# Holding back half of a back projection and placing it between the steps of the next memory attention

## The chip, the cores and the metric

One core of a Trainium2 chip runs the whole kernel. The metric is the device time in microseconds of one execution, and the lower is the better. The engines are PE (matmuls), PEld (its weight loads, which overlap), DVE (VectorE), ACT (ScalarE), POOL (GpSimd) and SP (it issues most DMAs).

## The reference

One block over 1024 tokens of width 1024, in fp32. Three residual stages follow one another:

```
x = x + mixer(norm(x)) @ w_out         8 heads with a top-256 index mask (DSA),
                                       8 heads with compressed, selected, window branches (NSA)
x = x + memory(norm(x), mem)           4 heads of 128 over 256 memory rows:
        q = rms(h @ w_xq); p = softmax(q k^T); o = p v; return o @ w_xo
x = x + square(relu(norm(x) @ w_ff_in)) @ w_ff_out      4096 features
```

The change lies in the second line: `o @ w_xo` is what the kernel calls the back projection, 512 columns in and 1024 out.

## The kernel before, in words

The tokens are eight tiles of 128 rows. After a head that projects the inputs, two streams of work are written out one between the other. `attend` is the mixer's attention, tile after tile. `fill` is everything else that can already be done: later projections, then `four_tiles` (L1207) for tiles 0 to 3, which adds the mixer's output projection (`rows_out`) and the memory attention, then their MLP, then tiles 4 and 5. What remains after the attention is the tail: `between` for tiles 6 and 7 and the MLP of tiles 4 to 7.

Both are Python generators that yield an amount of work after each piece. `together` (L122) takes a piece of `fill` as long as its sum is no more than the attention's sum times a pace, and else a piece of attention. A yielded pair such as `3, PACES[2]` is a gate: no more of `fill` is taken until the attention has begun the tile after that one, and the count starts again there. Gate 3 stands before `rows_out(3)`, since tile 3's attention output must be there. `alternate` (L156) takes from two streams in turn and `take` (L169) takes pieces of a stream until their sum reaches an amount. The result is only the order of the program: the tile scheduler (L81) moves each engine's instructions once more by a timeline of its own, so that the order on an engine is not the program's.

The memory attention of a pair of tiles is in `heads` (L1048). `w_xq` is multiplied first and leaves four items (two chunks of two heads for two tiles). `steps` then yields five times: after the transposes of all four, after the scores of chunk 0 (L1105 takes their maximum on DVE, L1109 the exponents on ACT), after those of chunk 1, and after the values of each chunk (L1126 transposes, L1141 copies). Score tiles and back projections both take the PSUM tag `D`, which has two banks.

The back projection is `made["xo", t0]`, a `gemm` (L385) with four chunks of 256 columns for two tiles, so eight items. Each is eight matmul records of whole fp32 on PE, 128x256, two groups of four (`psD<-wlo,xl`, `psD<-whi,xl`; the halves of a chunk's weights come raw into two rings, L314, 256 KB each), and one add into the residual rows on DVE (L1041). Each yields 4 x 4 x 256 / 2400 = 1.707.

The mixer's attention works at the same time. The top-k of its index (L770 to L772) is a chain on ACT: 32 bits per tile, each a pass over the scores (L770) and two one-column steps (L771, L772). L777 to L786 end it on DVE. In the stretches spoken of here it is tile 4's chain of 32, and its mask is needed only for tile 4's own DSA scores.

Of the kernel before, what the change touches and what calls it, by code (L numbers as in the profile page):

```python
# [155 lines left out]
def alternate(*streams):  # L156
    streams = list(streams)
    i = 0
    while streams:
        i %= len(streams)  # L160
        w = next(streams[i], None)
        if w is None:
            streams.pop(i)
        else:
            i += 1
            yield w


def take(gen, amount):  # L169
    done = 0.0  # L170
    while done < amount:
        w = next(gen, None)
        if w is None:
            return
        done += w
        yield w


def build(nc, tc, I, C, out):
# [21 lines left out]
    def ring(pool, tag, shape, dt=F32):  # L201
        n = RINGS[pool.name if isinstance(pool.name, str) else "dn"][tag]
        return pool.tile(shape, dt, tag=tag, name=tag, bufs=n)

    def row(ap):
        return ap[None, :]
# [71 lines left out]
    made, behind = {}, []  # L278
# [106 lines left out]
    def gemm(pool, xs, nk, nt, wsrc, chunks, consume, begun=None, keep=None, ks=None):  # L385

        for ci, parts in enumerate(chunks):
            w = sum(n for _, n in parts)
            gr = begun[ci] if begun and ci < len(begun) else list(
                weights(pool, xs, nk, wsrc, parts, None if keep is None else keep + ci, ks))  # L390
            for t in range(nt):
                pt = pst(TAGS[pool.name][0], [P, w])
                for i, k in enumerate(ks or range(nk)):
                    if len(xs) == 1:
                        mm(pt, xs[0](t, k), gr[i][0], i == 0, i == nk - 1)
                        continue
                    wh, wl = gr[i]
                    xh, xl = xs[0](t, k), xs[1](t, k)
                    mm(pt, xh, wh, i == 0, False)
                    mm(pt, xh, wl, False, False)  # L400
                    mm(pt, xl, wh, False, i == nk - 1)
                consume(ci, t, pt)
                yield nk * (5 - len(xs)) * w / 2400.0
# [9 lines left out]
    def xT(pool, nt, whole=False):  # L413

        parts = [pool.tile([P, DM // P, nt * P], F32 if whole else F32R, tag="x" + n, name="x" + n)
                 for n in ("h" if whole else "hl")]
        return (parts, [lambda t, k, x=x: x[:, k, t * P:(t + 1) * P] for x in parts],
                lambda t: [x[:, :, t * P:(t + 1) * P] for x in parts])
# [618 lines left out]
    def residual_add(x2):  # L1037
        def add_to(ci, t, pt):
            w = pt.shape[-1]
            dst = x2[t][:, ci * w:(ci + 1) * w]  # L1040
            v.tensor_tensor(dst, pt, dst, op=ALU.add)  # L1041
        return add_to

    def norm_of(*a):
        norm_T2(*a)
        yield 1.0
# [160 lines left out]
    def four_tiles(pool, x2, made):  # L1207

        four = [[(c * 256, 256)] for c in range(4)]
        room = pool.tile([P, 4, DM], F32, tag="xl", name="xl")  # L1210
        gb2 = [room[:, 3, c * 512:(c + 1) * 512] for c in range(2)]
        begun = {}

        def begin(t):
            o = room[:, t % 2].rearrange("p (k n) -> p k n", n=P)
            for c in (1, 0):
                nc.sync.dma_start(o[:, c * 4:c * 4 + 4, :], oT_dr[t][c])
            if t == 0:
                for u in range(2):
                    x2[u] = ring(pool, "b4", [P, DM])  # L1220
                    nc.sync.dma_start(x2[u], I["x"][0, u * P:(u + 1) * P, :])
                nc.sync.dma_start(room[:, 3], row(W["norm2_g"]).to_broadcast([P, DM]))
            elif t > 1:
                x2[t] = ring(pool, "b4", [P, DM])
                nc.sync.dma_start(x2[t], I["x"][0, t * P:(t + 1) * P, :])
            return [lambda _, k: o[:, k, :]]

        def add(t):
            return lambda ci, _, pt: residual_add(x2)(ci, t, pt)

        def rows_out(t, first=None):
            yield from gemm(pool, begin(t), 8, 1, W["w_out"], four, add(t), first, None, LAST_FIRST)

        def normed(t):
            return norm_of(pool, x2[t], gb2, xt_of(t))

        def memory_heads(t0):
            if t0 == 0:
                xo = room[:, 2].rearrange("p (k n) -> p k n", k=4)
                xo_of = lambda ci: xo[:, ci * 2:ci * 2 + 2, :]  # L1240
            else:
                xs = [ring(pool, "h", [P, 2, 2 * P]) for _ in range(2)]
                xo_of = lambda ci: xs[ci]
            consume_q, made["steps", t0] = heads(pool, 2, lambda ci: [xo_of(ci)], True)
            yield from gemm(pool, [lambda t, k: xf[0](t0 + t, k)], 8, 2, W["w_xq"], [[(0, 256)], [(256, 256)]], consume_q)
            rows = [lambda t, k: xo_of(k // 2)[:, k % 2, t * P:(t + 1) * P]]
            made["xo", t0] = gemm(pool, rows, 4, 2, W["w_xo"], four, lambda ci, t, pt: residual_add(x2)(ci, t0 + t, pt))

        mem_norms, keys, values = memory(pool)
        out0 = rows_out(0)  # L1250
        yield next(out0)
        yield from alternate(mem_norms, out0)
        _, xf, xt_of = xT(pool, 4, True)
        yield from keys
        yield from values
        yield 1, PACES[1]
        yield from alternate(rows_out(1), normed(0))
        yield from normed(1)
        yield from memory_heads(0)
        yield 2, PACES[2]  # L1260
        yield from alternate(made.pop(("steps", 0)), rows_out(2))
        yield from made.pop(("xo", 0))
        yield 3, PACES[2]
        yield from alternate(rows_out(3), normed(2))
        yield from normed(3)
        yield from memory_heads(2)
        yield from made.pop(("steps", 2))
        yield from alternate(made.pop(("xo", 2)), pre_norms(pool, made, x2))

    def pre_norms(pool, made, x2s):  # L1270

        made["x"] = xT(pool, 4)
        made["g"] = gain2(pool, W["norm3_g"])
        for t in range(2):
            yield from norm_of(pool, x2s[t], made["g"], made["x"][2](t))
# [302 lines left out]
    def fill():  # L1578
        for part in range(1, len(PARTS)):
            with tc.tile_pool(name="p2", bufs=1, reuse_waits="tile") as p2:  # L1580
                yield from project(p2, part, late, st)
            projected.append(part)
        pre_pool.__exit__(None, None, None)
        dn = dn_pool.__enter__()
        yield 0, PACES[0]
        x2s, made = {}, {}
        yield from four_tiles(dn, x2s, made)
        yield 3, PACES[3]
        yield from mlp(dn, 0, 4, x2s, made)
        yield 5, PACES[4]  # L1590
        rows = dn.tile([P, 2, 8 * 256], F32, tag="xh", name="xh")
        room = [rows[:, 0, :].rearrange("p (t k n) -> p t k n", t=2, k=8),
                dn.tile([P, 2, 8, 256], F32, tag="xl", name="xl"), rows[:, 1, :].rearrange("p (k n) -> p k n", k=8)]
        yield from between(dn, 4, 2, late["x2s"], False, None, room)
# [53 lines left out]
```

## Time and profile before

| | |
|---|---|
| median of 3 runs | 1666.52 us (1666.29 to 1670.05) |
| the profiled execution | 1667.92 us, span 1666.1 us |
| granted TensorE clock, mean | 0.992 |
| busy share of the span | PE 96%, PEld 85%, DVE 68%, ACT 67%, POOL 57% |
| DMA | 220.73 MB, 132 GB/s on average |

The share of PE says that almost any time won must come from one of the few stretches in which PE is not full. The windows of the trace show where these are; the waits and the timelines say what they wait for.

### The profile page before, as it was taken

Reading aid. Unit: us, or ns where it says so; the run is one execution under the profiler, and the core shown is the slowest. Engines: PE = TensorE matmul, PEld = TensorE weight load, DVE = VectorE, ACT = ScalarE, POOL = GpSimd, SP = SyncE. Lnnn points to the kernel's source line nnn. Section 1 sums busy time; section 2 is a strip of 40 time slices with the busy share of each in tenths; the row PEclk is TensorE's granted clock in tenths of the full one; section 3 lists DMA queues with packets and bytes.
Section 4 is the critical chain, followed back from the end, with each engine's and each line's share of the span. In section 5 each row is a group of like instructions: output and inputs, shape, how many; then the busy total and the mean of one; then the engine's idle time right before and its main releaser. Section 6 shows DMA issues by size and latency. Waiting matters only on the chain.

```text
span 1666.1 us, 29041 instructions
## 1 busy us (share of the span) xinstructions
PE 1604.1 (96%) x9602; PEld 1415.6 (85%) x9602; DVE 1127.0 (68%) x2590; ACT 1109.1 (67%) x2785; POOL 955.5 (57%) x1110
## 2 busy tenths in 40 slices
PE   6998998999999899999999999999998999999999
PEld 6998998788988798888888888888888997887887
DVE  5476779767776984475566665466668657888885
ACT  5455898896599769955998549883555554444443
POOL 2365568545543647777657867571245854554566
PEclk9999999999999999999999999999999999999999
DMA  7975423668444212222222222254268442332354
GB/s 257 307 264 161 149 83 110 227 180 251 135 137 148 78 45 75 78 70 75 70 79 64 69 69 72 71 175 136 86 223 253 150 147 89 103 101 93 100 168 149
DMA packets 184438, 220.73 MB, mean 132 GB/s; under 512 B 24672, under 2 KB 138208, under 8 KB 184288
## 3 DMA queue, kind: packets, MB, share of 16 engines
q1 hardware_dynamic: 176352, 208.39, 39.1%
q0 software_dynamic: 7936, 10.49, 2.4%
q8 instruction: 76, 1.25, 0.3%
q14 instruction: 74, 0.61, 0.1%
HBM read 186.58 MB, written 32.24 MB: 131 GB/s over the span
## 4 chain that ended last, share of the span: by engine, by line
PE 46%; DVE 6%; ACT 4%; POOL 3%; DMA 2%; issue 2%; SPq 0%; ACTq 0%; DVEq 0%; POOLq 0%
PE psD L234 22%; PE psS L234 9%; PE psM L234 5%; PE psPT L234 3%; PE psPV L234 3%; PE psPT L826 3%; POOL wlo L268 2%; DVE wlo L268 2%; DMA wraw<-in_w_ff_out_dram 1%; ACT dmask L770 1%; ACT whi L263 1%; DMA w<-in_w_ff_out_dram 1%; POOL S L816 0%; ACT S L811 0%; DVE P L1481 0%
## 5 line engine op out<-in xcount | busy, mean ns | idle before, releaser
L268 POOL TENSOR_TENSOR wlo<-wraw,whi 128x512 fp32r<-128x512 f32 (+1 forms) x228 | 316.7, 1395 | 198.3 <-ACT whi L263 192.1
L263 ACT ACTIVATE whi<-wraw 128x512 fp32r<-128x512 f32 x329 | 200.3, 626 | 178.0 <-DMA wraw<-in_w_ff_out_dram 37.9
L255 DVE TENSOR_TENSOR pl<-psPT,ph 128x512 fp32r<-128x512 f32 (+1 forms) x232 | 142.4, 620 | 64.8 <-ACT ph L254 63.0
L811 ACT ACTIVATE S<-S,mn 128x128 f32<-128x128 f32 (+7 forms) x192 | 143.1, 746 | 54.8 <-DVE mn L809 53.1
L234 PE MATMUL psD<-whi,h 128*128 128x512 f32 (+1 forms) x480 | 164.1, 397 | 0.5 <-POOL h L1395 0.2
L816 POOL TENSOR_SCALAR S<-S,sums,gi 128x640 f32<-128x640 f32 (+7 forms) x128 | 108.6, 857 | 86.4 <-DVE sums L814 65.8
L254 ACT ACTIVATE ph<-psPT 128x512 fp32r<-128x512 f32 (+1 forms) x232 | 122.9, 539 | 52.1 <-PE psPT L826 45.2
L234 PE MATMUL psD<-xh,wlo 128*128 128x512 f32 (+1 forms) x416 | 145.9, 352 | 0.0
L234 PE MATMUL psD<-xl,whi 128*128 128x512 f32 (+1 forms) x416 | 145.3, 351 | 0.0
L234 PE MATMUL psD<-xh,whi 128*128 128x512 f32 (+1 forms) x416 | 144.4, 352 | 0.3 <-ACT xh L254 0.3
L826 PE MATMUL psPT<-c_ident,S 128*128 128x128 f32 x816 | 133.0, 274 | 2.9 <-DVE ql L255 1.6
L234 PE MATMUL psD<-whi,xh 128*128 128x256 f32 (+1 forms) x512 | 130.4, 313 | 2.9 <-DMA whi<-W 2.3
L234 PE MATMUL psD<-wlo,xh 128*128 128x256 f32 (+1 forms) x512 | 131.0, 310 | 0.3 <-ACT relu L532 0.3
L268 DVE TENSOR_TENSOR wlo<-wraw,whi 128x512 fp32r<-128x512 f32 (+2 forms) x101 | 96.6, 963 | 48.6 <-ACT whi L263 44.6
L234 PE MATMUL psD<-whi,xl 128*128 128x256 f32 (+1 forms) x464 | 128.3, 319 | 0.0
L234 PE MATMUL psS<-K,qh 128*128 128x384 f32 (+3 forms) x288 | 108.2, 379 | 5.2 <-DVE mn L809 2.4
L826 PEld LDWEIGHTS psPT<-c_ident,S 128*128 128x128 f32 x816 | 98.3, 141 | 12.6 <-POOL S L816 2.7
L234 PEld LDWEIGHTS psD<-whi,h 128*128 128x128 f32 x480 | 89.9, 188 | 18.7 <-POOL h L1395 0.6
L234 PEld LDWEIGHTS psD<-whi,xh 128*128 128x128 f32 x512 | 92.2, 192 | 7.3 <-issue 1.7
L234 PE MATMUL psD<-wlo,h 128*128 128x512 f32 (+1 forms) x256 | 97.1, 394 | 0.3 <-DVE wlo L268 0.3
L234 PE MATMUL psS<-K,ql 128*128 128x384 f32 (+3 forms) x288 | 96.8, 340 | 0.0
L234 PEld LDWEIGHTS psD<-wlo,xh 128*128 128x128 f32 x512 | 91.8, 192 | 3.8 <-ACT relu L532 0.4
(407 smaller groups left out, 5021.4 us busy)
## 6 DMA issues: line engine op xcount, KB each, us to landing
wraw<-in_w_ff_in_dram SPq DMA_DIRECT2D x44, 512.0 KB, 3.8
wraw<-in_w_ff_in_dram SPq DMA_DIRECT2D x64, 256.0 KB, 2.7
wraw<-in_w_ff_out_dram SPq DMA_DIRECT2D x64, 256.0 KB, 2.6
wraw<-in_w_ff_out_dram SPq DMA_DIRECT2D x24, 512.0 KB, 4.5
w<-in_w_ff_out_dram SPq DMA_DIRECT2D x20, 512.0 KB, 5.4
wlo<-in_w_out_dram SPq DMA_DIRECT2D x36, 256.0 KB, 4.2
whi<-in_w_out_dram SPq DMA_DIRECT2D x36, 256.0 KB, 4.5
wraw<-in_w_in_dram SPq DMA_DIRECT2D x24, 256.0 KB, 4.7
```

The lines of the kernel that those rows point to most:

```text
L234: te.matmul(o, a, b, start=start, stop=stop)
L254: late["round"] = s.activation(hi, src, AF.Copy).ins
L255: late["split"] = v.tensor_tensor(lo, src, hi, op=ALU.subtract).ins
L263: s.activation(hi, raw, AF.Copy)
L268: (v if l == "v" else g).tensor_tensor(lo, raw, hi, op=ALU.subtract)
L770: s.activation(mask, src, AF.Sign, bias=c, accum_out=over)
L811: s.activation(S, S, AF.Exp, bias=low, scale=-1.0, accum_out=sums[:, hh:hh + 1])
L816: g.tensor_scalar(Ss[hh], Ss[hh], sums[:, hh:hh + 1], 1.0 if gate is None else gate[:, hh:hh + 1], op0=ALU.mult, op1=ALU.mult)
L826: te.transpose(p2[:, j, hh, :], S[:, (c + j) * P:(c + j + 1) * P], ident)
```

## The change

`xo` of tiles 0 and 1 was written out whole before gate 3. Now only pieces up to an amount of 6.0 go there, that is four of the eight items (4 x 1.707 = 6.83): chunks 0 and 1 for both tiles. The other four, chunks 2 and 3, are taken in turn with the five steps of tiles 2 and 3's memory attention.

```diff
         yield from memory_heads(0)
         yield 2, PACES[2]
         yield from alternate(made.pop(("steps", 0)), rows_out(2))
-        yield from made.pop(("xo", 0))
+        back = made.pop(("xo", 0))
+        yield from take(back, 6.0)
         yield 3, PACES[2]
         yield from alternate(rows_out(3), normed(2))
         yield from normed(3)
         yield from memory_heads(2)
-        yield from made.pop(("steps", 2))
+        yield from alternate(made.pop(("steps", 2)), back)
         yield from alternate(made.pop(("xo", 2)), pre_norms(pool, made, x2))
```

No instruction is added or removed. The order of each engine shows what moves. First PE, around the end of `xo` of tiles 0 and 1. `xl` with `wlo` or `whi` is the back projection, `psS`, `psPT`, `psPV` are the mixer's attention. Before, the eight items stand among the attention like this:

```order
L234 MATMUL psD<-wlo,xl 128x256 x2
L234 MATMUL psS<-K,qh 128x256
L234 MATMUL psS<-K,ql 128x256
L234 MATMUL psD<-whi,xl 128x256 x2
L234 MATMUL psPV<-ph,Vd 128x256
L234 MATMUL psPV<-pl,Vd 128x256
L234 MATMUL psPV<-ph,Vd 128x256
L234 MATMUL psPV<-pl,Vd 128x256
L234 MATMUL psPV<-ph,Vd 128x256
L234 MATMUL psD<-wlo,xl 128x256 x2
L234 MATMUL psD<-whi,xl 128x256 x2
L234 MATMUL psPV<-pl,Vd 128x256
```

In the changed order the fourth item ends at the first row below, and 33 rows of attention follow without a row of `psD`; the next is `rows_out(3)`:

```order
L234 MATMUL psD<-whi,xl 128x256 x2
L234 MATMUL psPV<-pl,Vd 128x256
L234 MATMUL psPV<-ph,Vd 128x256
L234 MATMUL psPV<-pl,Vd 128x256
L826 MATMUL psPT<-c_ident,S 128x128 x4
L716 MATMUL psPT<-c_ident,qd 128x128 x4
L234 MATMUL psS<-K,qh 128x256
L234 MATMUL psS<-K,ql 128x256
```

Before, that stretch of attention alone has 28 rows. The attention that stood between items 5 to 8 now stands alone.

Second, PE where the memory scores of tiles 2 and 3 are (`psD<-h` are score matmuls, then value matmuls). Before:

```order
L234 MATMUL psD<-h 128x256 x4
L234 MATMUL psPV<-pl,V_128 128x256
L234 MATMUL psPV<-ph,V_129 128x256
L826 MATMUL psPT<-c_ident,S 128x128 x4
L234 MATMUL psD<-h 128x256 x2
L234 MATMUL psPV<-pl,V_129 128x256
L234 MATMUL psPV<-ph,V_129 128x256
L234 MATMUL psPV<-pl,V_129 128x256
L826 MATMUL psPT<-c_ident,S 128x128 x2
L234 MATMUL psPV<-ph,V_129 128x256
```

And with the change, where an item of chunk 2 (tile 1) stands between the scores:

```order
L234 MATMUL psPV<-pl,V_129 128x256
L716 MATMUL psPT<-c_ident,qd 128x128 x4
L234 MATMUL psD<-wlo,xl 128x256 x2
L234 MATMUL psD<-whi,xl 128x256 x2
L334 MATMUL psM<-c_ident,relu 128x128 x2
L234 MATMUL psPV<-ph,V_129 128x256
L234 MATMUL psPV<-pl,V_129 128x256
L886 MATMUL psPT<-c_ident,cS_8115 128x128 x2
L234 MATMUL psD<-h 128x256 x6
```

The other three items stand 43 rows ahead of this one, and 17 and 25 rows behind it; the last two are between the transposes and the values.

Third, ACT in the first place, around the index transposes of tile 5 (`iqh`). `dmask,tko` is one bit of tile 4's top-k. Before:

```order
L770 ACTIVATE dmask,tko<-tkh,tkt 128x640
L771 ACTIVATE tks<-tko,tkg 128x1
L772 ACTIVATE tkt<-tks,tkt 128x1
L811 ACTIVATE S,sums<-S,mn 128x640
L838 ACTIVATE oc<-psPV 64x256
L770 ACTIVATE dmask,tko<-tkh,tkt 128x640
L254 ACTIVATE ph<-psPT 128x512
L771 ACTIVATE tks<-tko,tkg 128x1
L254 ACTIVATE iqh<-psPT 128x512
```

With the change:

```order
L770 ACTIVATE dmask,tko<-tkh,tkt 128x640
L811 ACTIVATE S,sums<-S,mn 128x640
L771 ACTIVATE tks<-tko,tkg 128x1
L838 ACTIVATE oc<-psPV 64x256
L254 ACTIVATE ph<-psPT 128x512
L772 ACTIVATE tkt<-tks,tkt 128x1
L254 ACTIVATE iqh<-psPT 128x512
L770 ACTIVATE dmask,tko<-tkh,tkt 128x640
```

Between the query transposes ahead (`qh`) and this `iqh`, ACT has seven bits of the chain before and five with the change; the other two follow later, and in both orders the 32nd bit stands right ahead of the first or second pair of memory exponents of tiles 2 and 3.

In the tail, `w_out` of tiles 6 and 7 has 192 rows (`psS<-whi,b`, `psS<-wlo,b`) ahead of the first row of the MLP's features on PE before, and 216 with the change.

## Rows read from the trace of the kernel before

**Rows 1.** The page's part 1: engine, busy us (share of the span), instructions.

```profile
span 1666.1 us, 29041 instructions
...
PE 1604.1 (96%) x9602; PEld 1415.6 (85%) x9602; DVE 1127.0 (68%) x2590; ACT 1109.1 (67%) x2785; POOL 955.5 (57%) x1110
```

**Rows 2.** Windows: us, busy of PE, PEld, DVE, ACT, POOL (instructions), clock, DMA share, GB/s.

```profile
484.00:504.00 20.00, 20.00 (x118) 18.15 (x118) 11.75 (x35) 19.20 (x56) 6.92 (x12) 1.00 0.46 138
504.00:513.00 9.00, 7.50 (x39) 6.25 (x38) 7.04 (x21) 8.09 (x22) 1.73 (x2) 0.81 0.45 132
513.00:545.00 32.00, 31.82 (x180) 28.83 (x179) 18.48 (x58) 30.70 (x87) 11.26 (x17) 1.00 0.45 138
545.00:571.00 26.00, 21.52 (x131) 18.01 (x131) 24.59 (x82) 19.97 (x57) 17.90 (x27) 0.93 0.31 90
571.00:592.00 21.00, 20.87 (x143) 19.49 (x142) 19.83 (x49) 13.98 (x32) 12.94 (x18) 1.00 0.14 44
592.00:1060.00 468.00, 465.30 (x2538) 400.26 (x2536) 283.27 (x649) 361.21 (x834) 317.10 (x322) 1.00 0.23 70
1264.00:1275.00 11.00, 6.09 (x34) 5.65 (x32) 8.71 (x9) 4.37 (x9) 6.63 (x4) 0.69 0.75 232
```

**Rows 3.** Groups of instructions by line and shape, 484 to 504 us; x is the count.

```profile
L234 PE MATMUL psD<-wlo,xl 128*128 128x256 f32 x32 | 8.2, 380 | 0.0
L234 PE MATMUL psD<-whi,xl 128*128 128x256 f32 x32 | 8.2, 379 | 0.0
...
L1041 DVE TENSOR_TENSOR b<-psD,b 128x256 f32<-128x256 f32 x7 | 2.9, 419 | 1.2 <-PE psD L234 1.1
```

**Rows 4.** Timeline of PE at 487 us: start, duration (both us), line, operation.

```profile
487.23 1.03 PE L234 MATMUL psD<-wlo,xl 128*128 128x256 f32 x4
488.10 1.03 PE L234 MATMUL psD<-whi,xl 128*128 128x256 f32 x4
488.96 0.49 PE L826 MATMUL psPT<-c_ident,S 128*128 128x128 f32 x3
```

**Rows 5.** Timeline of ACT at 490 us, two bits of the top-k.

```profile
490.06 0.83 ACT L770 ACTIVATE dmask<-tkh,tkt 128x640 bf16<-128x640 uint16 x1
...
491.67 0.83 ACT L770 ACTIVATE dmask<-tkh,tkt 128x640 bf16<-128x640 uint16 x1
```

**Rows 6.** Windows around the two stretches at a lower clock (columns of rows 2).

```profile
508.00:513.00 5.00, 4.52 (x21) 4.17 (x22) 4.41 (x13) 4.20 (x13) 0.00 (x0) 0.66 0.27 67
562.00:568.00 6.00, 4.92 (x22) 3.94 (x21) 5.13 (x18) 4.30 (x12) 3.99 (x7) 0.72 0.14 39
```

**Rows 7.** Waits of PE, 545 to 571 us: total, times, longest.

```profile
PE psPV L234 <- DVE pl L255: 1.7, 2, 1.4
PE psS L234 <- DVE S L807: 1.1, 1, 1.1
PE psM L334 <- DVE csum L875: 0.9, 1, 0.9
PE psS L234 <- ACT ir L738: 0.5, 1, 0.5
```

**Rows 8.** Timeline of DVE at 551 to 555 us.

```profile
551.38 1.48 DVE L783 TENSOR_TENSOR_SCAN tkl<-tkh 128x640 uint16<-128x640 bf16 x1
...
554.52 0.68 DVE L1105 TENSOR_REDUCE xnb<-psD 128x2 f32<-128x512 f32 x1
```

**Rows 9.** Timeline of PE, memory scores of tiles 2 and 3.

```profile
551.10 0.72 PE L234 MATMUL psD<-h 128*128 128x256 f32 x4
...
556.69 0.72 PE L234 MATMUL psD<-h 128*128 128x256 f32 x4
...
558.50 0.50 PE L234 MATMUL psD<-h 128*128 128x256 f32 x2
```

**Rows 10.** Timeline of ACT, the end of the exponents of a score tile.

```profile
558.25 0.21 ACT L1109 ACTIVATION_READ_ACCUMULATOR relu<-psD,xnb,xsc 128x1 f32 x1
```

**Rows 11.** Wait of PE in the tail, 1264 to 1275 us.

```profile
PE psS L234 <- DVE wlo L268: 4.9, 1, 4.9
```

## The prediction

> **What bounds the kernel.** I read the page's engine shares first. PE is busy for 1604.1 of 1666.1 us [rows 1], so 62.0 us of idle time in all is what an edit of the order can win, and there only in stretches where PE has holes. The windows say which. From 484 to 504 us, where the back projection of tiles 0 and 1 stands among the attention, PE is busy all 20.00 us and ACT 19.20: both are full. From 504 to 513, the attention alone ahead of gate 3, PE has 7.50 of 9.00 and a clock of 0.81. From 513 to 545 both are nearly full again (31.82 and 30.70 of 32). From 545 to 571, in the memory scores of tiles 2 and 3, PE has 21.52 of 26.00, ACT 19.97, but DVE 24.59. From 571 to 592 PE is full with DVE at 19.83 of 21. Behind that, up to 1060, PE has 465.30 of 468 [rows 2]. So the change takes PE work out of a place where PE and ACT are both full and puts it into one with 4.5 us of PE holes, in which DVE is the fullest engine. What the holes wait for is in the waits of that stretch: 1.7 us for the split `pl`, 1.1 for `S` and 0.9 for `csum`, all three from DVE, and 0.5 for `ir` from ACT [rows 7].
>
> **What is moved, and its size.** Nothing is added or removed. An item of the back projection is two groups of four records, each 0.87 us from its start to the start of what follows (487.23, 488.10, 488.96) [rows 4], so 1.73 us; the 32 and 32 records of the first stretch are eight items [rows 3]. Four move: 4 x 1.73 = 6.9 us of PE. With them go four adds of 0.42 us [rows 3], 1.7 us of DVE, and four weight loads of 256 KB on SP. These now stand behind the weights of `rows_out(3)` and `w_xq`; the DMA share is 0.46, 0.45 and 0.31 in the stretches concerned [rows 2], so I cost the loads at nothing: the cover is that the rings are filled ahead. If it is gone, PE waits for a load at the first moved item.
>
> **The first place: -3.4 us.** PE loses 6.9 us of work, but ACT does not. In 484 to 513 ACT is busy 19.20 + 8.09 = 27.3 of 29 us, 94% [rows 2]. What ACT does beside the attention is the chain of the top-k, whose bit takes 491.67 - 490.06 = 1.61 us back to back [rows 5], and the changed order of ACT has five bits where there were seven. ACT so loses 3.2 us: 27.3 - 3.2 = 24.1, and at the same 94% the stretch takes 25.6 us, 3.4 less. The two bits are not lost; they run later, and in both orders the chain ends right ahead of the first memory exponents, where ACT has 6.0 us free in 545 to 571 [rows 2]. The bounds are 0 (ACT or the attention's own chain sets the pace) and -6.9 (PE alone does). I take the value that ACT's row gives, since ACT is at 96% from 484 to 504 and PE only at 7.50 of 9.00 as soon as no back projection stands there.
>
> **The second place: +0.7 us.** 6.9 us of PE work meet 4.5 us of holes: +2.4. The clock is 0.72 in 562 to 568 [rows 6], which is 6 x 0.28 / 0.5 = 3.4 us at the lower level (1.2 GHz) and costs up to 1.7 us; it fell right behind the holes from 551 to 563, and with matmuls in them may not fall: 2.4 - 1.7 = +0.7. The bounds are 0 and +6.9, the latter if no hole takes any. DVE gets 1.7 us more in 47 us in which it is busy 44.4 [rows 2], so it has 2.6 us for that. It gains something too: the end of the top-k, with its scan of 1.48 us, stands ahead of a memory maximum (554.52, which waits some 2.7 us for its turn after the scores of 551.10 end at 551.82) [rows 8, 9], and follows later in the changed order. I count this as nothing, since the scan still has to run among the `pl` splits.
>
> **Rest.** The clock is 0.66 in 508 to 513 too [rows 6], the same 3.4 us at half speed. The attention alone grows from 28 to 33 rows with a lower load, so this may happen for longer; but PE waits there anyhow, so I count nothing, up to +1.7. The norms of tiles 0 and 1 for the MLP now need the adds of the last moved items, right ahead of them; eight items of tiles 2 and 3's back projection, 13.8 us, stand beside them as cover, so nothing; without it the price is one item and its add, 2.2 us. In the tail the order changes because the fill ran behind by another amount: 24 more rows of `w_out` stand ahead of the first feature row. PE has one wait of 4.9 us there for a split weight [rows 11], and a clock of 0.69 around it [rows 2]. This wait may go, stay or double: 0, between -4.9 and +4.9.
>
> **The sum.** -3.4 + 0.7 = -2.7 us. The profiled execution took 1667.92 us, 1.8 beside its span, and lies 1.4 above the median of 1666.52: 1667.9 - 2.7 - 1.4 = 1663.8, say **1664 us**.
>
> What a hole is worth hangs on which row is believed. The Trainium skill, page "Perfetto Trace Analysis", section "Identifying the Most-Contended Engine", holds that matmul busy time is a poor measure of how near a kernel is to its roofline, since pipelined matmuls overlap, and takes the busy share of weight loads instead. By PEld, 545 to 571 has 26 - 18.01 = 8.0 us free [rows 2], so that all 6.9 us would fit, and the sum would be -3.4 - 1.7 = -5.1, or 1661.4 us. I stay with PE's row, because eight back-to-back items show 0.87 us per group whatever their weight loads do.
>
> **Rival 1, it fits whole and the tail's wait goes** (chance 0.25). The items fall wholly into holes (0 in place of +2.4), the clock does not drop (-1.7), the first place gives -3.4 and the 4.9 us wait of the tail, whose place in the order is shifted by 24 rows, is covered: -10.0, or 1656.5 us; without the tail 1661.4. For it: most holes end on DVE, not on anything that the items need. Against it: two of the four items stand at transposes and values, behind the holes, where PE has 20.87 of 21 [rows 2].
>
> **Rival 2, ACT holds the first place, and it becomes slower** (chance 0.17). The place is the attention alone before gate 3. If ACT fills the room with further bits of the top-k or the chain of softmax, split and values has its own length, the stretch stays at 29 us whatever PE does: 0. The second place then pays whole: holes of 4.5 less the 1.7 that the adds put on DVE, the engine which ends them, take 2.8 of 6.9: +4.1. The longer stretch at half clock costs 1.7: +5.8, or 1672.3 us. It decides if the time from the first moved gap to `rows_out(3)` shrinks by less than 1 us. For it: ACT at 96% in the stretch. PE is also held up in order: the score matmul of 558.50 starts only when the exponent ending at 558.46 frees its bank of `D` [rows 9, 10], and an item among the scores takes such a bank for 1.73 + 0.42 us. The Trainium skill, page "TensorE: Matmul & The Clock Gate", section "Step-by-step: what each phase is for", states that only weight loads are pulled ahead and matmuls stay in program order, by which an item that waits for a bank would hold up the attention behind it; rows 9 and 10 agree, in that the score of 558.50 was waited for and nothing went past it. Against it: two bits did leave that place in the order, and they do so only as ACT's order shows.
>
> **Rival 3, nothing** (chance 0.08). The scheduler has already moved things so that what is won ahead of gate 3 is given back at the next gate, the MLP's, where attention must have reached tile 4's end: 1666.5 us. Against it: PE is the bound behind 592, with 2.7 idle us in 468 [rows 2], so a start that is earlier there is an earlier end.
>
> **How the numbers follow.** About 0.3%, 5.0 us, is what a measurement of this kernel can tell from no change. The forecast has 0.50; its own range is 1660 to 1667, and 0.06 of it lies below 1661.5. Faster: 0.25 + 0.06 = 0.31. Same: 0.44 + 0.08 = 0.52. Slower: 0.17. The range reaches from Rival 1 with the whole tail, 1656, to just short of Rival 2, 1672, which leaves out some 0.05 below and 0.10 above.
>
> **What would show it.** Right: 484 to `rows_out(3)` is 3 to 4 us shorter with PE's holes larger there; the window of the memory scores grows by 1 to 3 us with PE busy above 90%; `S <- DVE` and `pl <- DVE` waits of PE shrink; behind it the trace is shifted by 2 to 3 us as a whole. Wrong: the first place is not shorter (Rival 2), or the window of the scores is not longer (Rival 1), or the start of the long MLP stretch is shifted by another amount than the end, which then is the tail.

## The result and the profile after

The change takes **1678.85 us** (median; 1678.14 to 1682.96) where the kernel before took 1667.91 in the same comparison: a ratio of 1.0065, 95% interval 1.004 to 1.009. It is about 11 us slower, where 1664 us had been forecast and 1672 was the upper end.

The page of the changed kernel's profile, first part:

```profile
span 1677.1 us, 29056 instructions
...
PE 1603.4 (96%) x9602; PEld 1415.1 (84%) x9602; DVE 1128.4 (67%) x2590; ACT 1110.2 (66%) x2785; POOL 964.1 (57%) x1110
```

PE's busy time is what it was (1604.1 before [rows 1]), the span is 11.0 us longer. So the whole loss is idle time of PE: 62.0 us before, 73.7 with the change. (The 15 more instructions of the page are in none of the five engines' counts.) Some of the windows of rows 2, of the changed kernel:

```profile
484.00:504.00 20.00, 17.88 (x111) 15.38 (x110) 13.44 (x41) 19.53 (x56) 8.67 (x14) 1.00 0.42 127
...
545.00:571.00 26.00, 22.24 (x137) 19.37 (x136) 23.40 (x73) 20.11 (x57) 16.92 (x27) 0.95 0.36 110
571.00:592.00 21.00, 20.55 (x130) 19.09 (x129) 19.20 (x48) 12.23 (x29) 11.18 (x14) 0.98 0.08 22
592.00:1060.00 468.00, 462.72 (x2528) 397.51 (x2526) 289.40 (x657) 363.38 (x837) 321.69 (x323) 1.00 0.22 69
```

The first window, full before, now has 2.1 us of holes, and ACT is still full (19.53). The window of the memory scores has PE at 22.24 of 26, hardly more than the 21.52 before [rows 2]. From 592 to 1060 there are 5.28 us of holes and not 2.70. None of that is 11 us. To see where it arises, the same instructions have to be looked up in both traces: an early matmul of the back projection (480 us), the first of `rows_out(3)` behind gate 3 (512), and one of tiles 2 and 3's back projection, behind all that was moved (591). The timeline of PE (start, duration, line, operation; what it waited for in brackets), before:

```profile
480.80 0.38 PE L234 MATMUL psD<-whi,xl 128*128 128x256 f32 x1
...
512.49 1.09 PE L234 MATMUL psD<-wlo,xl 128*128 128x256 f32 x4
...
591.00 1.03 PE L234 MATMUL psD<-wlo,h 128*128 128x256 f32 x4
```

and after:

```profile
480.28 1.03 PE L234 MATMUL psD<-whi,xl 128*128 128x256 f32 x4
...
505.21 1.13 PE L234 MATMUL psD<-wlo,xl 128*128 128x256 f32 x4 [0.75 <-DMA xl<-o]
...
588.25 1.03 PE L234 MATMUL psD<-wlo,h 128*128 128x256 f32 x4
```

The three stand 0.5, 7.3 and 2.8 us earlier. So the first place is 6.8 us shorter, the second cost 4.5, and at the third row the fill is 2.2 us ahead, 107.97 us behind the first row and not 110.20, near what was forecast. The windows between these rows (columns of rows 2), before and then after:

```profile
480.80:512.49 31.69, 30.19 (x170) 26.79 (x169) 21.45 (x64) 30.14 (x82) 10.82 (x17) 0.95 0.45 135
512.49:591.00 78.51, 73.71 (x447) 65.89 (x447) 62.35 (x188) 64.01 (x172) 41.22 (x60) 0.98 0.32 98
```

```profile
480.28:505.21 24.93, 22.05 (x133) 18.80 (x131) 18.25 (x54) 24.41 (x68) 10.85 (x17) 1.00 0.43 131
505.21:588.25 83.04, 78.82 (x473) 71.19 (x474) 65.40 (x189) 66.47 (x184) 39.27 (x57) 0.98 0.35 105
```

They warn against reading 2.2 us as time won. PE's idle time between the first and the third row is 6.3 us before and 7.1 with the change. And in these stretches PE has run 302 rows of attention before and 291 with the change: the fill is ahead in part because attention comes later. Now the first row of the MLP's features in the tail, before and after:

```profile
1274.46 0.28 PE L234 MATMUL psD<-xh,whi 128*128 128x256 f32 x1
```

```profile
1281.85 0.28 PE L234 MATMUL psD<-xh,whi 128*128 128x256 f32 x1
```

It is 7.4 us late. 24 more rows of `w_out` stand ahead of it, at 0.12 us each 2.9 us that need not be done later; the rest is lost, and more behind it. From 1228 to 1420 us, the waits of PE before (total, times, longest):

```profile
PE psS L234 <- DVE wlo L268: 4.9, 1, 4.9
PE psD L234 <- DVE b L1041: 1.2, 1, 1.2
PE psPT L334 <- DVE relu L360: 1.0, 1, 1.0
```

and after:

```profile
PE psPT L334 <- DVE relu L360: 6.4, 3, 4.3
PE psS L234 <- ACT h L254: 3.5, 1, 3.5
PE psD L234 <- DVE b L1041: 1.2, 1, 1.2
```

Before, PE stands once for 4.9 us; after, it waits for the norms of tiles 6 and 7 (`relu`, L360) three times and for their transposed memory queries (`h`). This window holds 3.8 of the 11.7 us of new idle time, the largest part; 592 to 1060 holds 2.6, 1420 to 1520 holds 2.0, and the rest is in smaller pieces. In the queue of SP the residual rows of tiles 4 and 5, which the features need, go out and come back later. Before:

```profile
1241.96 0.42 SPq L1205 DMA_DIRECT2D x<-b  x1
...
1245.04 0.34 SPq L1205 DMA_DIRECT2D x<-b  x1
...
1247.68 0.49 SPq L1354 DMA_DIRECT2D b<-x  x1
...
1249.92 0.73 SPq L1354 DMA_DIRECT2D b<-x  x1
```

After, with two loads of `w_xq` between the read-backs:

```profile
1244.30 0.34 SPq L1205 DMA_DIRECT2D x<-b  x1
...
1247.33 0.34 SPq L1205 DMA_DIRECT2D x<-b  x1
...
1249.41 0.51 SPq L1355 DMA_DIRECT2D b<-x  x1
...
1250.82 1.52 SPq L273 DMA_DIRECT2D wraw<-in_w_xq_dram  x2
1252.70 0.34 SPq L1355 DMA_DIRECT2D b<-x  x1
```

### The profile page after: what moved, and what is told of

It reads as the page before. It is cut to its first block, busy times and chain, and to the rows that moved or that the text cites. A ratio compares the mean times of both kernels' runs of the same rounds, so it can differ in the third digit from the quotient of the medians.

```text
span 1677.1 us, 29056 instructions
## 1 busy us (share of the span) xinstructions
PE 1603.4 (96%) x9602; PEld 1415.1 (84%) x9602; DVE 1128.4 (67%) x2590; ACT 1110.2 (66%) x2785; POOL 964.1 (57%) x1110
## 4 chain that ended last, share of the span: by engine, by line
PE 63%; DVE 10%; DMA 7%; ACT 7%; POOL 6%; issue 6%; SPq 1%; POOLq 0%; ACTq 0%; DVEq 0%
PE psD L234 33%; PE psS L234 11%; PE psM L234 5%; PE psPT L234 4%; PE psPV L234 4%; PE psPT L826 4%; POOL wlo L268 2%; DMA wraw<-in_w_in_dram 1%; DVE wlo L268 1%; POOL S L816 1%; DMA wraw<-in_w_ff_out_dram 1%; ACT dmask L770 1%; ACT whi L263 1%; ACT S L811 1%; DVE S L809 1%
## 5 line engine op out<-in xcount | busy, mean ns | idle before, releaser
L263 ACT ACTIVATE whi<-wraw 128x512 fp32r<-128x512 f32 x329 | 201.6, 626 | 195.5 <-PE psD L234 40.5
```

The lines of the kernel that those rows point to most:

```text
L263: s.activation(hi, raw, AF.Copy)
```

## The experiments

The suspicion is that the loss is no work of the moved items at all. Four items less ahead of gate 3 mean that all later work of the fill stands further back against the attention, and so the order at the end of the attention is another one. The order of PE bears out the first half: by the 301st feature row of the first MLP, PE has run 824 rows of attention with the change and 804 before, counted from the first row above. The amounts at which the fill is taken can be set without touching the change: by the last two numbers of `PACES`, the pace beside the MLP and the pace beside tiles 4 and 5. With them, PE's order in the tail of one kernel can be given to the other.

**The change with the tail of before.**

```diff
 # the change
-PACES = (1.5, 1.35, 1.35, 1.75, 1.75)
+PACES = (1.5, 1.35, 1.35, 1.75, 2.2)
```

> The change, with the last pace at 2.2 in place of 1.75, so that the fill has caught up at the end of the attention and PE's order of the tail is that of the kernel before (192 rows of w_out ahead of the first feature row, not 216). Theory 1, the loss is the order of the tail: in the change's trace, PE at 611 us of the kernel before stood 2.7 us earlier, and the loss came behind 1239 us. So this kernel keeps the 2.7 us and is 2 to 4 us faster than the kernel before (about 1665 us), 13 us faster than the change. Theory 2, the loss comes from the moved items themselves (adds, bank D, residual rows that are done later, felt in the MLP): it stays 8 to 11 us slower than the kernel before.

Measured: 1669.08 us, ratio to the kernel before 1.0004 (0.9992 to 1.0016). The loss is gone: the moved items do not make the 11 us. The 2.7 us that were to stay are not there either.

**The kernel before with the tail of the change.**

```diff
 # the kernel before
-PACES = (1.5, 1.35, 1.35, 1.75, 1.75)
+PACES = (1.5, 1.35, 1.35, 1.75, 1.6)
```

> The kernel before, not one item moved, with the last pace at 1.6, which leaves the fill behind at the end of the attention and gives PE the tail's order of the change, row by row. Theory 1, the tail's order: 9 to 14 us slower than the kernel before, about 1679 us, with PE's long waits on L360 and on h at the start of the tail. Theory 2, the moved items: within 3 us of the kernel before.

Measured: 1680.10 us, 1.0075 (1.0058 to 1.0091). The kernel before, with no item moved, is as slow as the change once it has the change's tail. Its waits of PE from 1228 to 1420 us are also the change's:

```profile
PE psPT L334 <- DVE relu L360: 6.9, 3, 4.0
PE psS L234 <- ACT h L254: 3.5, 1, 3.5
PE psD L234 <- DVE b L1041: 1.6, 1, 1.6
```

Theory 2 falls by both runs, and Theory 1 holds in the size of the loss: 12.8 us here, 9.8 between the change and the change with the old tail.

**The kernel before with that pace.**

```diff
 # the kernel before
-PACES = (1.5, 1.35, 1.35, 1.75, 1.75)
+PACES = (1.5, 1.35, 1.35, 1.75, 2.2)
```

> The kernel before with the last pace at 2.2 and nothing else: what the pace alone does to the stretch of tiles 4 and 5, with the tail's order of PE as before. Both theories: within 2 us of the kernel before. If it is several us faster or slower, the pace and not the moved items stands behind the first of these runs.

Measured: 1667.99 us, 1.0009 (0.9997 to 1.0022). The pace by itself does nothing that can be told, so the first run compares with this one: 1.0004 against 1.0009. With the same tail, the change makes no difference that these intervals show.

**The items beside rows_out(3).**

```diff
 # the change, last pace 2.2
-        yield from alternate(rows_out(3), normed(2))
+        yield from alternate(rows_out(3), normed(2), back)
         yield from normed(3)
         yield from memory_heads(2)
-        yield from alternate(made.pop(("steps", 2)), back)
+        yield from made.pop(("steps", 2))
```

> The four items held back as in the change, but put beside rows_out(3), right behind gate 3, where PE had 31.82 of 32 us, and not between the steps of the memory attention; last pace 2.2, tail as before. If the second place takes the items in its holes, this kernel pays for them in full behind the gate and keeps the holes: 3 to 5 us slower than the kernel that has them between the steps. If the place behind the gate does not matter: within 1 us of it.

Measured: 1670.74 us, 1.0022 (1.0008 to 1.0036), 1.7 us above the kernel with the items between the steps. That lies between the two expectations, and the intervals of the two kernels overlap. So it is not settled whether the holes between the steps are worth anything; the 3 to 5 us that were expected if they took the items did not show.

**How far the tail's order matters.** Four more settings of the two paces give other numbers of `w_out` rows ahead of the first feature row.

```diff
 # the change
+PACES = (1.5, 1.35, 1.35, 1.9, 2.2)      24 rows
 # the kernel before
+PACES = (1.5, 1.35, 1.35, 1.9, 2.2)      26 rows
 # the change
+PACES = (1.5, 1.35, 1.35, 1.8, 2.2)      134 rows
 # the change
+PACES = (1.5, 1.35, 1.35, 1.6, 1.75)     288 rows
```

> The change with the last two paces at 1.9 and 2.2: the fill is further ahead at the end of the attention, and PE's order has 24 rows of w_out ahead of the first feature row of the tail (192 in the kernel before, 216 with the change). Theory A, the later the features start against w_out of tiles 6 and 7, the less work stands beside the chains of these tiles and the more is lost: 4 us or more faster than the kernel before. Theory B, only the order with 216 rows happens to be a bad one, there is no trend: within 4 us of the kernel before, on either side.

> The kernel before with the last two paces at 1.9 and 2.2, no item moved: 26 rows of w_out ahead of the first feature row. Both theories as for the kernel with 24 rows, and the two within 3 us of one another, since the moved items themselves cost and give nothing that lasts.

> The change with the last two paces at 1.8 and 2.2: 134 rows of w_out ahead of the first feature row. Theory A: between the kernel with 24 rows and the change with the tail as before, so 0 to 5 us faster than the kernel before. Theory B: within 4 us of the kernel before, with no order among the three.

> The change with the last two paces at 1.6 and 1.75: the fill further behind, 288 rows ahead of the first feature row. Theory A: slower than the change, 1683 us or more. Theory B: anything between 1664 and 1685 us, the change not the worst.

| rows of `w_out` ahead | kernel | us | ratio to before |
|---|---|---|---|
| 24 | change | 1680.87 | 1.0074 (1.0057 to 1.0091) |
| 26 | before | 1683.06 | 1.0094 (1.0079 to 1.0109) |
| 134 | change | 1664.16 | 0.9984 (0.9970 to 0.9997) |
| 192 | before | 1667.34 | 1 |
| 192 | change, first run above | 1669.08 | 1.0004 (0.9992 to 1.0016) |
| 216 | change as it is | 1678.85 | 1.0065 (1.004 to 1.009) |
| 216 | before, second run above | 1680.10 | 1.0075 (1.0058 to 1.0091) |
| 288 | change | 1691.75 | 1.0144 (1.0128 to 1.0160) |

From 134 rows on the order is Theory A's: the later the features start, the longer the kernel. Only the step from 134 to 192 rows is not clear of noise for the change, which took 1667.29 us in a second run with 134 rows, below. Theory A falls at 24 and 26 rows, where 4 us of gain were expected and 13 to 16 us of loss came. Theory B falls too: it had both of these within 4 us of the kernel before, and 288 rows at 1685 us or less. The windows from 1228 to 1420 us say the same as the times. Each line is one kernel: busy PE, PEld, DVE, ACT, POOL, then clock, DMA share, GB/s. Before:

```profile
1228.00:1420.00 192.00, 182.66 (x1163) 164.61 (x1164) 131.08 (x194) 100.57 (x199) 114.06 (x110) 0.98 0.56 180
```

The change, 216 rows:

```profile
1228.00:1420.00 192.00, 178.86 (x1137) 161.84 (x1136) 119.78 (x185) 99.00 (x194) 109.76 (x108) 0.96 0.54 170
```

288 rows:

```profile
1228.00:1420.00 192.00, 174.81 (x1123) 159.77 (x1122) 113.22 (x181) 94.66 (x193) 103.68 (x109) 0.93 0.50 157
```

24 rows:

```profile
1228.00:1420.00 192.00, 169.66 (x1115) 154.16 (x1114) 127.82 (x186) 100.88 (x197) 116.16 (x109) 0.95 0.55 174
```

PE's idle time in these 192 us is 9.3, 13.1, 17.2 and 22.3 us, and the clock is lower in all three than before (0.96, 0.93 and 0.95 against 0.98), though not in the order of the idle time. What PE waits for differs. With 288 rows it is the chain of the memory queries of tiles 6 and 7:

```profile
PE psS L234 <- DVE relu L1090: 6.6, 2, 5.9
PE psS L234 <- ACT h L254: 2.5, 1, 2.5
```

With 24 rows it is one wait:

```profile
PE psS L234 <- ACT b L263: 15.5, 1, 15.5
```

`b` of L263 is tile 6's or 7's attention output, split by ACT. The fill has run out ahead of the attention's end, and PE has nothing but the work that needs this output. The wait runs from 1233.1 us, where the attention's last row on PE ends, to 1248.6: the output still has to go to memory and come back, as the queue of SP shows:

```profile
1234.38 0.59 SPq L840 DMA_DIRECT2D o<-oc  x1
...
1240.24 1.72 SPq L1155 DMA_DIRECT2D wraw<-o  x2
```

So there are two ways to be wrong: too much fill done leaves the way behind the attention's end alone, too little leaves the chains of tiles 6 and 7 alone.

**The tail of 134 rows in both kernels.** Is the 134-row kernel faster by its tail, or by the change?

```diff
 # the kernel before
+PACES = (1.5, 1.35, 1.35, 1.79, 1.75)
 # the change
+PACES = (1.5, 1.35, 1.35, 1.8, 1.75)
```

> The kernel before, no item moved, with the last but one pace at 1.79: PE's order of the tail is, row by row, that of the change with 134 rows, which was 3 us faster than the kernel before. If that gain is the tail's alone, this kernel has it too: 1664 us, within 1.5 us of the change with 134 rows. If the moved items have a share, the 2 to 3 us that the first two places won: 1666 to 1668 us.

> The change with the last but one pace at 1.8 and the last as it was (1.75): the tail's order of 134 rows once more, to stand beside the kernel before with that tail. By the moved items' own gain 1664 us, 2 to 3 us ahead of the other; without one, both the same.

Measured: the kernel before 1663.28 us, 0.9970 (0.9956 to 0.9984); the change 1667.29, 1.0001 (0.9986 to 1.0015). PE's order of the tail is the same in both, row by row. So the gain is the tail's, as the first expectation had it; the moved items add none, and here the change is 4.0 us slower. The window from 1228 to 1420 us of the kernel before with 134 rows has the least idle time of PE of all, 6.4 us:

```profile
1228.00:1420.00 192.00, 185.56 (x1172) 166.87 (x1171) 138.23 (x205) 103.78 (x201) 121.02 (x112) 0.98 0.59 189
```

This kernel is also the version that beats both: 1.0065 / 0.9970, some 0.9% under the change and 0.3% under the kernel before, for one number.

## Why the prediction was wrong

The direction was wrong and the time lay outside the range. By its steps:

- **The first place, forecast at -3.4 us, measured at -6.8.** The step said that ACT, at 94%, sets the pace. ACT stayed full (19.53 of 20 in the changed kernel's first window), and yet the stretch shrank by nearly all that PE lost. What filled ACT was mostly the chain of the top-k; of its 19.20 us from 484 to 504 before, these groups make 14.1:

```profile
L770 ACT ACTIVATE dmask<-tkh,tkt 128x640 bf16<-128x640 uint16 x9 | 7.4, 825 | 0.2
...
L772 ACT ACTIVATE tkt<-tks,tkt 128x1 f32<-128x1 f32 x9 | 2.6, 291 | 0.2
L771 ACT ACTIVATE tks<-tko,tkg 128x1 f32<-128x1 f32 x9 | 2.6, 290 | 0.2
...
L770 ACT ACTIVATION_READ_ACCUMULATOR dmask<-tkh,tkt 128x1 f32 x8 | 1.5, 188 | 0.0
```

  Nothing needs its result until tile 4's own scores, so its bits ran at other moments: 12 passes of L770 start between the two rows before, and 9 with the change. The bound of -6.9, "PE alone", was nearly the right value, and not by chance: the orders of PE, ACT, DVE and POOL are the same this far in kernels that differ only by the last two paces, and the stretch takes 31.5 to 31.7 us in five traces with the order of before and 24.8 to 25.0 in six with the change.
- **The second place, forecast at +0.7, measured at +4.5.** The 4.5 is high by a fall of the clock behind the holes in this one execution (0.95 and 0.98 in 545 to 571 and 571 to 592). Four of the other kernels with the same order have no such fall, and take 81.5 to 82.0 us from the second row to the third; the order of before takes 78.2 to 78.8 in five. So the place costs about 3 to 4 us. Two parts of the term were mis-sized. The clock did stay up in the holes, but that was priced at 1.7 us, and the order of before takes only 0.3 to 0.6 us less in the two traces in which the clock stays up as well (78.18, against 78.43 to 78.77). And the holes took little: PE's idle time from 545 to 571 shrank from 4.5 to 3.8 us. In the changed kernel PE still waits there, by the waits from 545 to 571 us:

```profile
PE psD L234 <- ACT relu L1109: 1.1, 1, 1.1
PE psS L234 <- DVE mn L809: 1.0, 2, 0.8
PE psPT L826 <- POOL S L816: 1.0, 1, 1.0
PE psPV L234 <- DVE pl L255: 0.6, 1, 0.6
```

  The 1.1 us is an item itself, which waits for a score tile's bank until the exponents are done, as Rival 2 had it. The reading by weight loads, by which all 6.9 us fit (the Trainium skill, "Perfetto Trace Analysis", "Identifying the Most-Contended Engine"), is further off than PE's row: 8.0 us free by PEld, 4.5 by PE, and 0.7 us less idle time afterwards. In this stretch the waits decide, not the room on an engine.
- **The sum of the two, forecast at -2.7, measured at -2.2.** The number is near by luck: both terms were off, by amounts that cancel. And it is not all time won, by PE's idle time and the 11 rows of attention that come later (under the result).
- **"PE is the bound behind 592, with 2.7 idle us in 468 [rows 2], so a start that is earlier there is an earlier end"** (against Rival 3). It failed too: from 592 to 1060 us the idle time of PE grew from 2.70 to 5.28 us, with waits for POOL that the kernel before does not have there, as these:

```profile
PE psD L234 <- POOL h L1321: 0.9, 1, 0.9
PE psD L234 <- POOL wlo L268: 0.7, 1, 0.7
PE psM L234 <- POOL wlo L268: 0.7, 2, 0.4
```

  That is about what the fill was ahead, so it was given back. The mix there is another one: between the first and the 301st feature row stand 504 rows of attention, and 481 before. That this is the cause was not tried by itself; with the same tail the change came out at 1.0004 against 1.0009 in one pair and 1.0001 or 0.9984 against 0.9970 in the other, so it gives nothing and may cost a few us.
- **The tail, forecast at "0, between -4.9 and +4.9".** This is the step that failed: a term put at nothing, and bounded too narrowly. It was bounded by the one wait that the kernel before shows there, as if only that wait could go or double. The new order made new ones: first 6.4 us in three waits for the norms and 3.5 us for `h`, and a lower clock around them (0.96 in place of 0.98, though the mean over the whole kernel is 0.993 and was 0.992). Measured by the pairs with exchanged tails it is worth 9.8 to 12.8 us, twice the upper bound or more. The text had seen the 24 rows that moved; it priced them by the trace of an order that was no longer there.
- The rivals: Rival 2 had the sign, but neither its place nor its reason; the first place did not hold. The local gain was given back later, as in Rival 3, but no run shows that the gate that it names does it. The prediction did name the sign that came: the first feature row of the MLP is 1.8 us earlier (599.84 against 601.60), that of the tail 7.4 us later.

Shown by the runs: the loss sits in the order of the tail, for each kernel and with either set of items. Argued, not shown: which link of that order starts it. The trace has the write and read-back of tiles 4 and 5's residual rows 2 to 3 us late and two `w_xq` loads ahead of it; no run moved these alone.

## What to carry to other kernels

When an order is made from amounts and gates, work that is put behind a gate shifts all that follows against the other stream, up to the place where that stream ends. A row of one stream that comes earlier is no gain until it is known what the other stream has done by then. Look first at the place where the stream ends: what runs beside the last chains, and is it still there? Price a new order by what will stand alone in it, not by the waits of the old one, and try the pace first, since one number (the pace beside the MLP at 1.6 or at 1.8, 1691.75 against 1667.29 us) moved the change by 24 us, where the edit itself won nothing that lasts.

## What the runs showed of the hardware

Before, TensorE's clock fell in the stretch of attention alone: 0.81 with PE at 7.50 of 9.00 us busy [rows 2]. With the change it stayed up there. The window of this stretch in the changed kernel:

```profile
497.50:506.50 9.00, 7.37 (x40) 5.42 (x41) 7.54 (x21) 8.92 (x25) 2.04 (x3) 1.00 0.22 61
```

It would be easy to put this down to the change, since ahead of it PE was busy 20.00 of 20 us before and 12.26 of 13.5 with the change. But the second experiment, the kernel before with the tail of the change, has the order of before in this stretch. PE is busy all 13.50 of 13.5 us ahead of the stretch, and the clock stays up all the same:

```profile
505.50:514.50 9.00, 6.79 (x39) 4.99 (x38) 7.50 (x22) 8.70 (x23) 1.73 (x2) 1.00 0.43 132
```

Of the five traces with this order two have the fall to the lower level (1.2 GHz) here and three have not, so one trace does not tell whether an edit removed it. Nor was it worth much where PE waits anyhow: from 480.80 to 512.49 us, or between the same two rows, the stretch takes 31.69 us in both traces with the fall and 31.49 to 31.61 in the three without. So the +1.7 us that the prediction held possible here would have been at most 0.2. Where PE is full it costs more: the second place of the change takes 83.0 us in the two traces with a fall in it and 81.5 to 82.0 in the four without. Why the clock falls in one execution and not in another was not tried.
